# The recurrent mixer of the second block: one inversion of all small blocks, and four solving chains in lock step

## The chip, the cores and the metric

The kernel runs on one core of one Trainium2 chip. What counts is the device time of one execution in microseconds (us); the median of three runs stands for a kernel. One more execution was taken with the profiler, and all durations below come from it. The TensorE clock of the core has two levels here, 1.2 and 2.4 GHz; the profile gives the granted share of the higher one.

## The reference, cut to what matters

The program is a whole two-layer first block, then a second block. In the second block three parts share the input: a recurrent mixer (RWKV-7), a latent attention, and two gates over both. Their merge goes on to a router and 32 experts.

```python
def step(state, inp):                       # recurrent mixer, one token, 8 heads of 64
    r_t, w_t, k_t, v_t, kk_t, a_t = inp
    sa = jnp.einsum('bhvk,bhk->bhv', state, -kk_t)
    state = (state * w_t[:, :, None, :]
             + sa[..., None] * (kk_t * a_t)[:, :, None, :]
             + v_t[..., None] * k_t[:, :, None, :])
    return state, jnp.einsum('bhvk,bhk->bhv', state, r_t)
...
y = (y - mean) * lax.rsqrt(var + GN_EPS)    # per head, then weight and bias
y = (y + bonus) * g
...
merged = gate_rw * (y_rw @ w_branch_rw[l]) + gate_mla * (y_mla @ w_branch_mla[l])
x = x + merged @ w_out[l]
```

The kernel computes the 512 steps in 8 pieces of 64 tokens. Within a piece the tokens depend on each other through a unit triangular 64x64 matrix per head, whose inverse is needed; it is put together from the inverses of its two diagonal 32x32 blocks and one correction. With 8 heads, 8 pieces and 2 blocks there are 128 such small blocks. Between pieces a 64x64 state is carried on.

## The kernel before

Two heads share a tile of 128 partitions, so there are four chains, numbered `ct` 0 to 3.

`prepare` (L1307) makes a chain's operands in two halves of 4 pieces each, so it runs eight times: decay sums and exponentials, `KR` and its partners, products between them on the PE (L1292), transposes (L126), evictions split between ScalarE and VectorE (L1402, L1404). After the second half it stores the chain's triangular matrices (`nd`, L1376) and loads their 32 small blocks as rows of the tile `NB` (L1381), one block a partition: chain `ct` has partitions 32 ct to 32 ct + 31.

`invert` (L1415) inverts the blocks of two chains, so 64 partitions, by 31 steps of two VectorE instructions: an outer product (L1422) and a subtraction (L1424), of up to 256 elements a partition. It then stores the inverses to DRAM (`xbd`, L1427, a DMA that GpSimd's queue issues) and loads them as blocks into the tiles `TT` (L1433, four loads a chain, on the sync queue SP). It is written as a generator, and the caller advances it between other steps: chains 0 and 1 are inverted during the last four runs of `prepare`, chains 2 and 3 while chains 0 and 1 are solved.

`solve` (L1437) takes one chain from the inverses to the output. It loads `rt`, `bon` and `gg`; transposes the first blocks (`T1`, L1454); makes the off-diagonal block by two rounds of 32x32 products (L1460, L1470); multiplies the inverse with `R` (wide products through `products`, L1292), which gives `W` and `Zn`; makes `Phi`, `Psi`, `rt`; then runs the recursion over 6 pieces (product in `pairmm`, L1285, sum on VectorE, L1501); makes `y` (L1507, L1509, L1512); and normalises it with two products with `mean64` (L1515, L1523), a logarithm and an exponential on ScalarE (L1524, L1525), and seven VectorE passes, of which the last splits `y` into two parts, `yrh` and `yrl` (L359, L360). It yields after each step.

`merge_work` (L1556) is the work that depends on none of this: 4 projections of gate columns, then 4 latents with a gate projection and a product with the latent attention's output; in all 80 steps of 6 products (L188 to L190), 480 products of 128x512. VectorE evicts gates at L1538 and merges latents at L1551, which GpSimd's queue stores (L1552, L1559). The first 54 steps (`FREE`, L1296) are free to run at any time. The other 26 are bound: `solve_pair` (L1565) goes round its two chains, and after every second solving step ties one step of six products behind that solving step (`issue_after`, L1578). Chains 0 and 1 are solved first, then 2 and 3 (L1611, L1614).

The order of the instructions on each engine is made by a scheduler at build time from this program order; on the chip each engine takes its instructions in that order. Behind the mixer comes the merge: 96 products with `w_branch_rw` (L1672 to L1674), 48 of which need chains 0 and 1 and 48 chains 2 and 3, then the output projection, the router and the experts.

Of the kernel before, what the change touches and what calls it, by code (L numbers as in the profile page):

```python
# [9 lines left out]
F32 = mybir.dt.float32  # L10
# [5 lines left out]
OP = mybir.AluOpType  # L16
PSUM = bass.MemoryType.PSUM

T = 512
# [62 lines left out]
def build(tc, A, out):  # L82
    nc = tc.nc
# [24 lines left out]
    tt = nc.vector.tensor_tensor  # L108
# [1165 lines left out]
    def rwkv():  # L1274
        with tc.tile_pool(name="rw", bufs=1) as rp:
# [138 lines left out]

            def invert(cts, eng):  # L1415

                rows = slice(32 * cts[0], 32 * cts[0] + 64)
                N_, X_ = NB[rows], XB[rows]
                for j in range(31):
                    n_ = 31 - j  # L1420
                    o = outer[rows, :(j + 1) * n_].rearrange("p (s t) -> p s t", t=n_)
                    eng.tensor_tensor(o, X_[:, 0:j + 1, j:j + 1].to_broadcast([64, j + 1, n_]),  # L1422
                       N_[:, j:j + 1, j + 1:].to_broadcast([64, j + 1, n_]), OP.mult)
                    eng.tensor_tensor(X_[:, 0:j + 1, j + 1:], X_[:, 0:j + 1, j + 1:], o, OP.subtract)  # L1424
                    yield
                xbd = scratch.tile([64, 32, 32], F32, name=f"xbd{cts[0]}")
                nc.gpsimd.dma_start(xbd, X_)  # L1427
                for i, ct in enumerate(cts):
                    for h in range(2):
                        for hb in range(2):  # L1430
                            r0 = 64 * h + 32 * hb
                            p0 = 32 * i + 16 * h + 8 * hb
                            nc.sync.dma_start(TT[ct][r0:r0 + 32, :, 32 * hb:32 * hb + 32],  # L1433
                                                xbd[p0:p0 + 8].rearrange("c s t -> s c t"))
                yield

            def solve(sp, ct):  # L1437
# [4 lines left out]

                def tmp(nm):
                    return sp.tile([128, T], F32, tag=f"stmp{ct % 2}", name=nm, bufs=5)

                def load(nm, src):
                    t_ = sp.tile([128, T], F32, tag="s_" + nm, name=nm, bufs=2)
                    nc.sync.dma_start(t_, src)
                    return t_
                rt = c8(load("rt", rtd[ct].rearrange("p c t -> p (c t)")))  # L1450
                bon, gg = load("bon", bond[ct]), load("gg", ggd[ct])
                t_ = tmp("T1")
                T1, Z2 = c8(t_[:, 0:256]), c8(t_[:, 256:])
# [21 lines left out]

                W = c8(tmp("W"))
                Zn = c8(tmp("Zn"))
                for hf in range(2):
# [5 lines left out]
                    act(Zn[:, 4 * hf:4 * hf + 4], pv[:, :, 1], AF.Copy, scale=-1.0)  # L1484
                Phi = c8(tmp("Phi"))
                tt(Phi, id2[:, None].to_broadcast([128, 8, 64]), dec[:, :, None].to_broadcast([128, 8, 64]),
                   OP.mult)
                yield last
                for l_, r_, dst, op in ((W, Btok, Phi, OP.subtract), (Btok, Zn, Psi, OP.add),
# [4 lines left out]
                    yield last  # L1494
                M = c8(tmp("M"))
                nc.vector.tensor_copy(M[:, 1], Psi[:, 0])
# [13 lines left out]

                y = tmp("y")
                tt(c8(y), c8(p), Y0, OP.add)  # L1512
# [3 lines left out]
                tt(y, y, pm, OP.subtract)  # L1516
                sq = tmp("sq")
                sqi = act(sq, y, AF.Square)
# [45 lines left out]

            def solve_pair(a, b, side, steps):  # L1565

                nonlocal todo
                gens = [a, b]
                while gens:
                    for g in list(gens):  # L1570
                        last = next(g, None)
                        if last is None:
                            gens.remove(g)
                            continue
                        todo += RATE
                        while todo >= 1.0:
                            todo -= 1.0
                            with tc.issue_after(last.ins):  # L1578
                                next(work, None)
                        for _ in range(steps):  # L1580
                            next(side, None)
            outer = rp.tile([128, 256], F32, name="outer")
# [14 lines left out]
            with tc.tile_pool(name="rw_prepare", bufs=1) as pp:  # L1597
                inv = invert((0, 1), nc.vector)
                for i in range(8):
                    for _ in prepare(pp, i // 2, i % 2):  # L1600
                        if i >= 4:
                            next(inv, None)
                            next(inv, None)
                for _ in inv:
                    pass
            for _ in range(FREE):
                next(work)
            with tc.tile_pool(name="rw_solve", bufs=1) as sp:
                inverse_tiles(sp, (2, 3))
                inv = invert((2, 3), nc.vector)  # L1610
                solve_pair(solve(sp, 0), solve(sp, 1), inv, 2)  # L1611
                for _ in inv:
                    pass
                solve_pair(solve(sp, 2), solve(sp, 3), iter(()), 0)  # L1614
            for _ in work:
# [517 lines left out]
```

## Time and profile before

| | |
|---|---|
| median of three runs | 2293.4 us (2291.48 to 2294.9) |
| the profiled execution | 2294.18 us, span of the trace 2292.4 us |
| busy over the span | PE 2110.6 us (92%), weight loads 1661.8, VectorE 1691.4 (74%), ScalarE 1312.1, GpSimd 701.2 |
| the preparation | 1600 to 1729 us from the start of the span |
| solving | 1730 to 1829 us |
| merge of the branches | 1829 to 1853 us |
| experts | from about 1940 us |

PE is TensorE's matmul part, PEld its weight loads, DVE VectorE, ACT ScalarE, POOL GpSimd, SP the sync engine, which only issues DMAs. Times of events count from the start of the span. The ends of matmuls are modelled in the trace, so their spacing (from start to start) is read, not their duration. A `q` behind an engine's name is its queue of waits and DMA issues.

### The profile page before, as it was taken

How to read it: one execution, taken by the hardware profiler on the slowest of the kernel's cores; microseconds unless marked ns; L12 is line 12 of the kernel's file. 1: busy time of each engine (PE TensorE's matmuls, PEld its weight loads, DVE VectorE, ACT ScalarE, POOL GpSimd, SP SyncE). 2: the span in 40 equal slices, each digit the busy share in tenths (PEclk: the TensorE clock that was granted, in tenths of full speed). 3: DMA queues.
4: the chain of work that ended last, by engine and by line, in shares of the span. 5: the costliest groups of instructions: out<-in, count | busy, mean ns of one | idle time of the engine just before them, and what ended most of it. 6: DMA issues, size and time to landing. Idle time of an engine off the chain costs nothing. (4 is left out here: it accounts for less than half of the span.)

```text
span 2292.4 us, 31372 instructions
## 1 busy us (share of the span) xinstructions
PE 2110.6 (92%) x11354; PEld 1661.8 (72%) x11354; DVE 1691.4 (74%) x2725; ACT 1312.1 (57%) x2018; POOL 701.2 (31%) x620
## 2 busy tenths in 40 slices
PE   7798899999999799899999998999899996999995
PEld 6676688778777677678777876577667775777663
DVE  6888884766686888894676685475697565899897
ACT  4454664544555345764555456776763433888884
POOL 1343421233232444421223232332232042222214
PEclk9999999999999899899999999999999997999997
DMA  5211218566633112127666636556786695999992
GB/s 149 63 56 45 78 47 221 153 159 166 169 89 124 38 56 83 53 40 222 169 156 154 174 84 177 146 116 171 208 198 163 176 345 179 315 321 333 312 341 115
DMA packets 236547, 364.56 MB, mean 159 GB/s; under 512 B 46983, under 2 KB 135431, under 8 KB 234336
## 3 DMA queue, kind: packets, MB, share of 16 engines
q1 hardware_dynamic: 183952, 270.96, 36.3%
q0 software_dynamic: 32048, 84.30, 17.0%
q10 hardware_dynamic: 20384, 7.21, 1.3%
q8 instruction: 92, 1.51, 0.3%
q14 instruction: 71, 0.58, 0.1%
HBM read 302.78 MB, written 40.14 MB: 150 GB/s over the span
## 5 line engine op out<-in xcount | busy, mean ns | idle before, releaser
L879 DVE TENSOR_TENSOR wlo<-draw,whi 128x1024 fp32r<-128x1024 f32 x112 | 189.4, 1694 | 165.0 <-ACT whi L878 165.0
L161 ACT ACTIVATE whi<-wraw 128x1024 fp32r<-128x1024 f32 x171 | 179.2, 1054 | 203.5 <-PE ps_g L189 87.9
L1985 DVE TENSOR_TENSOR wlo<-eraw,whi 128x1024 fp32r<-128x1024 f32 x190 | 229.7, 1235 | 34.5 <-ACT whi L1984 31.0
L167 DVE TENSOR_TENSOR wlo<-wraw,whi 128x1024 fp32r<-128x1024 f32 x132 | 171.8, 1307 | 60.3 <-ACT whi L161 59.8
L1984 ACT ACTIVATE whi<-eraw 128x1024 fp32r<-128x1024 f32 x190 | 197.2, 1072 | 30.9 <-PE ps_s L1910 22.4
L188 PE MATMUL ps_g<-uh,whi 128*128 128x512 f32 x512 | 199.7, 390 | 0.0
L190 PE MATMUL ps_g<-uh,wlo 128*128 128x512 f32 x512 | 199.7, 390 | 0.0
L189 PE MATMUL ps_g<-ul,whi 128*128 128x512 f32 x512 | 199.6, 390 | 0.0
L878 ACT ACTIVATE whi<-draw 128x1024 fp32r<-128x1024 f32 x112 | 118.1, 1054 | 103.8 <-PE ps_g L189 73.3
L190 PE MATMUL ps_g<-h2h,wlo 128*128 128x512 f32 (+1 forms) x288 | 117.8, 410 | 2.5 <-DMA wlo<-wraw 2.5
L188 PE MATMUL ps_g<-hhh,whi 128*128 128x512 f32 x288 | 117.3, 408 | 2.0 <-ACT whi L170 1.8
L188 PE MATMUL ps_g<-h2h,whi 128*128 128x512 f32 (+1 forms) x288 | 118.8, 413 | 0.3 <-DMA wlo<-wraw 0.3
L189 PE MATMUL ps_g<-h2l,whi 128*128 128x512 f32 (+1 forms) x288 | 117.8, 409 | 0.0
L190 PE MATMUL ps_g<-hhh,wlo 128*128 128x512 f32 x288 | 117.6, 408 | 0.0
L189 PE MATMUL ps_g<-hhl,whi 128*128 128x512 f32 x288 | 116.2, 404 | 0.0
L563 POOL TENSOR_TENSOR KE<-Dm,kk 128x512 f32<-128x512 f32 x56 | 78.0, 1403 | 108.5 <-ACT Dm L561 63.5
L188 PEld LDWEIGHTS ps_g<-uh,whi 128*128 128x128 f32 x512 | 96.2, 188 | 20.3
L190 PEld LDWEIGHTS ps_g<-uh,wlo 128*128 128x128 f32 x512 | 96.2, 188 | 20.2
L189 PEld LDWEIGHTS ps_g<-ul,whi 128*128 128x128 f32 x512 | 96.2, 188 | 20.0
L840 ACT ACTIVATE ar<-ps_g 128x512 f32<-128x512 f32 x64 | 38.0, 593 | 125.6 <-PE ps_g L190 125.6
L854 POOL DMA_DIRECT2D draw<-in_w_down_dram x16 | 21.2, 1327 | 285.9 <-DMA draw<-in_w_down_dram 127.1
L1909 PE MATMUL ps_s<-wlo,xth 128*104 128x512 f32 x256 | 105.7, 413 | 2.0 <-DVE wlo L1985 1.8
(774 smaller groups left out, 6185.5 us busy)
## 6 DMA issues: line engine op xcount, KB each, us to landing
eraw<-in_moe_w_gu_dram SPq DMA_DIRECT2D x61, 1024.0 KB, 17.7
draw<-in_w_down_dram SPq DMA_DIRECT2D x40, 1024.0 KB, 5.9
wraw<-in_w_in_dram SPq DMA_DIRECT2D x74, 512.0 KB, 3.8
wraw<-in_w_up_dram SPq DMA_DIRECT2D x64, 512.0 KB, 5.2
eraw<-in_moe_w_down_dram SPq DMA_DIRECT2D x30, 1024.0 KB, 17.8
wlo<-wraw POOLq DMA_DIRECT2D x39, 512.0 KB, 5.5
draw<-in_w_down_dram POOLq DMA_DIRECT2D x16, 1024.0 KB, 9.3
draw<-draw POOLq DMA_DIRECT2D x16, 1024.0 KB, 7.1
```

The costliest lines, as they stand in the source:

```text
L161: act(hv, rv, AF.Copy)
L167: tt(lv, rv, f32(hv), OP.subtract)
L188: mm(o, hi[:, j, cs], xh, start=(k == 0), stop=False)
L189: mm(o, hi[:, j, cs], xl, start=False, stop=False)
L190: mm(o, lo[:, j, cs], xh, start=False, stop=(k == K - 1))
L563: nc.gpsimd.tensor_tensor(KE, Dm.rearrange("p c b u m -> p (c b u m)"), kk, OP.mult)
L840: act(ar[:, 2 * s:2 * s + 2, c], p.rearrange("p (i t) -> p i t", i=2), AF.Relu)
L878: act(hi, rv, AF.Copy)
L879: tt(lo, rv, f32(hi), OP.subtract)
L1909: mm(pg, XTh[:, k], lo[:, j], start=False, stop=False)
L1984: act(hi, rv, AF.Copy)
L1985: tt(lo, rv, f32(hi), OP.subtract)
```

## The change

All 128 blocks are inverted by one pass of 62 instructions over 128 partitions, after the whole preparation and ahead of the free steps of `merge_work` in program order. The inverses are stored by two DMAs and loaded by sixteen. All four chains are then solved in one round. Each chain has two tiles of its own (`tp`, `my`) in place of five from a ring: `W` and `Zn` are written into `R`, `T1`, `Z2`, `Phi` and the squares share `tp`, `M` and `y` share `my`. `rt` has four buffers, `bon` and `gg` keep two for four chains.

```diff
-            def invert(cts, eng):
-                rows = slice(32 * cts[0], 32 * cts[0] + 64)
-                N_, X_ = NB[rows], XB[rows]
+            def invert():
                 for j in range(31):
                     n_ = 31 - j
-                    o = outer[rows, :(j + 1) * n_].rearrange("p (s t) -> p s t", t=n_)
-                    eng.tensor_tensor(o, X_[:, 0:j + 1, j:j + 1].to_broadcast([64, j + 1, n_]),
-                       N_[:, j:j + 1, j + 1:].to_broadcast([64, j + 1, n_]), OP.mult)
-                    eng.tensor_tensor(X_[:, 0:j + 1, j + 1:], X_[:, 0:j + 1, j + 1:], o, OP.subtract)
-                    yield
-                xbd = scratch.tile([64, 32, 32], F32, name=f"xbd{cts[0]}")
-                nc.gpsimd.dma_start(xbd, X_)
-                for i, ct in enumerate(cts):
+                    o = outer[:, :(j + 1) * n_].rearrange("p (s t) -> p s t", t=n_)
+                    tt(o, XB[:, 0:j + 1, j:j + 1].to_broadcast([128, j + 1, n_]),
+                       NB[:, j:j + 1, j + 1:].to_broadcast([128, j + 1, n_]), OP.mult)
+                    tt(XB[:, 0:j + 1, j + 1:], XB[:, 0:j + 1, j + 1:], o, OP.subtract)
+                xbd = scratch.tile([128, 32, 32], F32, name="xbd")
+                for i in range(2):
+                    nc.gpsimd.dma_start(xbd[64 * i:64 * i + 64], XB[64 * i:64 * i + 64])
+                for ct in range(4):
...
-                def load(nm, src):
-                    t_ = sp.tile([128, T], F32, tag="s_" + nm, name=nm, bufs=2)
+                t_, my = [sp.tile([128, T], F32, name=f"{nm}{ct}") for nm in ("tp", "my")]
+                def load(nm, src, bufs):
+                    t_ = sp.tile([128, T], F32, tag="s_" + nm, name=nm, bufs=bufs)
...
-                rt = c8(load("rt", rtd[ct].rearrange("p c t -> p (c t)")))
-                bon, gg = load("bon", bond[ct]), load("gg", ggd[ct])
-                t_ = tmp("T1")
+                rt = c8(load("rt", rtd[ct].rearrange("p c t -> p (c t)"), 4))
+                bon, gg = load("bon", bond[ct], 2), load("gg", ggd[ct], 2)
...
-                W = c8(tmp("W"))
-                Zn = c8(tmp("Zn"))
+                W, Zn = R[:, :, 0], R[:, :, 1]
...
-            def solve_pair(a, b, side, steps):
+            def solve_all(gens):
                 nonlocal todo
-                gens = [a, b]
...
-                        for _ in range(steps):
-                            next(side, None)
...
             with tc.tile_pool(name="rw_prepare", bufs=1) as pp:
-                inv = invert((0, 1), nc.vector)
                 for i in range(8):
                     for _ in prepare(pp, i // 2, i % 2):
-                        if i >= 4:
-                            next(inv, None)
-                            next(inv, None)
-                for _ in inv:
-                    pass
-            for _ in range(FREE):
-                next(work)
+                        pass
             with tc.tile_pool(name="rw_solve", bufs=1) as sp:
                 inverse_tiles(sp, (2, 3))
-                inv = invert((2, 3), nc.vector)
-                solve_pair(solve(sp, 0), solve(sp, 1), inv, 2)
-                for _ in inv:
-                    pass
-                solve_pair(solve(sp, 2), solve(sp, 3), iter(()), 0)
+                invert()
+                for _ in range(FREE):
+                    next(work)
+                solve_all([solve(sp, ct) for ct in range(4)])
```

The lines above shift by a few in the changed kernel: the outer product is L1420 there, the subtraction L1422, the gate eviction L1532, the latent's merge L1545, the first block product L1455, the second L1465, the loads of a chain L1444. Three places show what the scheduler made of it.

On VectorE, in the preparation of the third chain, before (a row is the line, the operation, output and inputs, and the output's shape; `SB` and `SK` are evictions of the preparation, `outer` and `inverses` the inversion):

```order
L1340 SCALAR_TENSOR_TENSOR kk<-zk,k_k,sq 128x256
L1424 TENSOR_TENSOR inverses<-inverses,outer 64x4x28
L1371 TENSOR_TENSOR SB_12862<-ps_m,past 128x512
L1422 TENSOR_TENSOR outer<-inverses,blocks 64x135
L1371 TENSOR_TENSOR SK<-ps_m,past 128x512
L1424 TENSOR_TENSOR inverses<-inverses,outer 64x5x27
L1385 TENSOR_TENSOR km<-km,dec_12866 128x256
```

and now, at the end of the preparation:

```order
L1404 COPY KV<-ps_m 64x2x64 x2
L1404 COPY Btok_12869<-ps_m 64x2x64 x2
L1532 TENSOR_TENSOR gate<-ps_g,Rb_10846 128x512
L1545 SCALAR_TENSOR_TENSOR gate<-gate,ps_g 128x512 x2
L1420 TENSOR_TENSOR outer<-inverses,blocks 128x31
L1422 TENSOR_TENSOR inverses<-inverses,outer 128x31
L1420 TENSOR_TENSOR outer<-inverses,blocks 128x60
```

The inversion no longer alternates with the preparation; its 62 instructions stand behind it and behind the first latent's merges, with two gate evictions between them and the transposes of `TT` behind.

On the PE, at the start of solving, now (`ymh`, `yml` and `wlo` are operands of work products, `tp` the transposed blocks of a chain; 71 work products in a row end with the first three rows, where before there were 37):

```order
L188 MATMUL ps_g<-ymh,whi 128x512
L189 MATMUL ps_g<-yml,whi 128x512
L190 MATMUL ps_g<-ymh,wlo 128x512
L1455 MATMUL ps_s<-tp_14476,SB_12852 32x32 x16
L1455 MATMUL ps_m<-tp_14504,SB_12857 32x32 x16
...
L1455 MATMUL ps_s<-tp_14538,SB_12862 32x32 x16
L1465 MATMUL ps_s<-TT_12893,tp_14476 32x32 x16
L1465 MATMUL ps_s<-TT_13905,tp_14538 32x32 x16
L1292 MATMUL ps_s<-R_12853,TT_12893 64x128 x11
L1455 MATMUL ps_m<-tp_14566,SB_12867 32x32 x16
```

Where "..." stands are six work products. All four chains' first products now follow the free work; six work products stand between most pairs of steps from there on, and after the last pair the eight products with `mean64` and the merge follow with none between.

On the sync queue, where the merge's operands are loaded, now (`gates` takes the stored gates `gd` and latents `partd`; `bon` and `gg` are the bonus and output gate of chains 2 and 3):

```order
L1643 DMA gates<-gd 128x512 x2
L155 DMA wraw<-in_w_out_dram 128x2x512 x2
L1643 DMA gates<-partd 128x512 x2
L1444 DMA bon<-bond 128x512 x2
L1444 DMA gg<-ggd 128x512 x2
L1757 DMA yd<-zero 128x1024 x2
```

Before, those four loads stood directly behind the loads of `TT` for chains 2 and 3, ahead of all loads of `gates`.

## Rows read from the trace of the kernel before

**Rows 1.** Busy time by stretch: each engine busy (instructions), clock, DMA share, GB/s.

```profile
core 0: us, PE busy (x) PEld busy (x) DVE busy (x) ACT busy (x) POOL busy (x), PEclk, DMA share, GB/s
1621.20:1626.60 5.40, 5.37 (x37) 4.78 (x38) 3.73 (x8) 3.66 (x5) 2.08 (x4) 0.50 1.07 276
...
1621.00:1685.00 64.00, 62.44 (x588) 49.20 (x588) 50.51 (x138) 51.64 (x109) 21.48 (x37) 0.95 0.73 188
1685.00:1730.00 45.00, 40.15 (x368) 30.90 (x368) 40.75 (x126) 25.56 (x56) 17.39 (x26) 1.00 0.78 186
...
1940.00:2230.00 290.00, 286.79 (x1382) 203.74 (x1381) 261.42 (x302) 255.47 (x360) 71.02 (x56) 1.00 0.95 322
```

**Rows 2.** Waits of the PE, 1685 to 1730: us in total, times, longest.

```profile
PE ps_m L1292 <- ACT KV L1402: 1.9, 3, 1.2
PE ps_m L1292 <- DVE za L1364: 1.7, 1, 1.7
PE ps_m L1292 <- ACT y0b L1411: 1.2, 1, 1.2
```

**Rows 3.** Waits of the PE, 1738 to 1828.

```profile
PE ps_s L1285 <- DVE M L1501: 1.2, 2, 0.7
```

**Rows 4.** Timeline of the PE: start, duration, engine, line, operation, count.

```profile
1729.04 0.28 PE L1292 MATMUL ps_m<-KV,SK 64*64 64x64 f32 x2
...
1737.52 0.39 PE L188 MATMUL ps_g<-ymh,whi 128*128 128x512 f32 x1
1737.74 0.40 PE L189 MATMUL ps_g<-yml,whi 128*128 128x512 f32 x1
1738.07 0.69 PE L1460 MATMUL ps_s<-T,SB 32*32 32x32 f32 x32
```

**Rows 5.** Timeline of GpSimd's queue: stores of the inverses, loads of the blocks.

```profile
1723.68 0.57 POOL L1427 DMA_DIRECT2D xbd<-inverses  x1 [2.29 <-DVE inverses L1424]
1724.27 2.73 POOL L1381 DMA_DIRECT2D blocks<-nd  x4
...
1777.14 0.58 POOL L1427 DMA_DIRECT2D xbd<-inverses  x1 [8.78 <-DVE M L1501]
```

**Rows 6.** DMAs by tile: queue, count, size, median us from issue to landing.

```profile
partd<-gate POOLq DMA_DIRECT2D x8, 256.0 KB, 4.3
...
bon<-bond SPq DMA_DIRECT2D x4, 256.0 KB, 4.5
blocks<-nd POOLq DMA_DIRECT2D x16, 32.0 KB, 4.9
```

**Rows 7.** VectorE by line, 1737.9 to 1777: busy us, mean ns, idle before.

```profile
L1424 DVE TENSOR_TENSOR inverses<-inverses,outer 64x31 f32<-64x31 f32 (+15 forms) x31 | 10.5, 339 | 1.0
L1422 DVE TENSOR_TENSOR outer<-inverses,blocks 64x31 f32<-64x31 f32 (+15 forms) x31 | 10.5, 339 | 1.0
```

**Rows 8.** Timeline of VectorE: transposes of chains 0, 1 and 2.

```profile
1730.80 0.45 DVE L1454 STREAM_TRANSPOSE T<-TT 128x256 f32<-128x256 f32 x1 [3.51 <-DMA TT<-xbd]
1735.03 0.45 DVE L1454 STREAM_TRANSPOSE T<-TT 128x256 f32<-128x256 f32 x1 [3.78 <-DMA TT<-xbd]
...
1785.99 0.44 DVE L1454 STREAM_TRANSPOSE T<-TT 128x256 f32<-128x256 f32 x1
```

**Rows 9.** Timeline of the sync queue: loads of the blocks, chains 0 and 1.

```profile
1726.72 4.83 SPq L1433 DMA_DIRECT2D TT<-xbd  x8
```

**Rows 10.** Timeline of the PE: first wide products of chain 0 and of chain 2.

```profile
1742.24 3.60 PE L1292 MATMUL ps_s<-R,TT 64*64 64x128 f32 x31 [0.79 <-ACT TT L1473]
...
1795.88 2.04 PE L1292 MATMUL ps_s<-R,TT 64*64 64x128 f32 x31
```

**Rows 11.** Timeline of the PE: mean products of chains 0 and 1.

```profile
1784.32 1.02 PE L1515 MATMUL ps_s<-y,mean 128*128 128x512 f32 x2
1785.18 1.02 PE L1515 MATMUL ps_m<-y,mean 128*128 128x512 f32 x2
```

**Rows 12.** Timeline of VectorE: splits that end chains 0 and 1.

```profile
1795.65 0.69 DVE L360 TENSOR_TENSOR yrl<-y,yrh 128x512 fp32r<-128x512 f32 x1 [0.45 <-ACT yrh L359]
...
1798.12 0.69 DVE L360 TENSOR_TENSOR yrl<-y,yrh 128x512 fp32r<-128x512 f32 x1 [0.57 <-ACT yrh L359]
```

More of the change, by code (lines that the diff above doesn't have):

```diff
@@ L1431, in invert @@
                             r0 = 64 * h + 32 * hb
-                            p0 = 32 * i + 16 * h + 8 * hb
+                            p0 = 32 * ct + 16 * h + 8 * hb
                             nc.sync.dma_start(TT[ct][r0:r0 + 32, :, 32 * hb:32 * hb + 32],
                                                 xbd[p0:p0 + 8].rearrange("c s t -> s c t"))
-                yield
             def solve(sp, ct):
@@ L1441, in solve @@
                 tag = "sm"[ct % 2]
-                def tmp(nm):
-                    return sp.tile([128, T], F32, tag=f"stmp{ct % 2}", name=nm, bufs=5)
-                def load(nm, src):
-                    t_ = sp.tile([128, T], F32, tag="s_" + nm, name=nm, bufs=2)
+                t_, my = [sp.tile([128, T], F32, name=f"{nm}{ct}") for nm in ("tp", "my")]
+                def load(nm, src, bufs):
+                    t_ = sp.tile([128, T], F32, tag="s_" + nm, name=nm, bufs=bufs)
                     nc.sync.dma_start(t_, src)
                     return t_
-                rt = c8(load("rt", rtd[ct].rearrange("p c t -> p (c t)")))
-                bon, gg = load("bon", bond[ct]), load("gg", ggd[ct])
-                t_ = tmp("T1")
+                rt = c8(load("rt", rtd[ct].rearrange("p c t -> p (c t)"), 4))
+                bon, gg = load("bon", bond[ct], 2), load("gg", ggd[ct], 2)
                 T1, Z2 = c8(t_[:, 0:256]), c8(t_[:, 256:])
@@ L1484, in solve @@
                     act(Zn[:, 4 * hf:4 * hf + 4], pv[:, :, 1], AF.Copy, scale=-1.0)
-                Phi = c8(tmp("Phi"))
+                Phi = c8(t_)
                 tt(Phi, id2[:, None].to_broadcast([128, 8, 64]), dec[:, :, None].to_broadcast([128, 8, 64]),
@@ L1494, in solve @@
                     yield last
-                M = c8(tmp("M"))
+                M = c8(my)
                 nc.vector.tensor_copy(M[:, 1], Psi[:, 0])
@@ L1509, in solve @@
                             last = mm(o, M[h, c], rt[h, c], start=False, stop=True)
-                y = tmp("y")
+                y = my
                 tt(c8(y), c8(p), Y0, OP.add)
@@ L1516, in solve @@
                 tt(y, y, pm, OP.subtract)
-                sq = tmp("sq")
+                sq = t_
                 sqi = act(sq, y, AF.Square)
```

## The prediction

> **What bounds the kernel now.** I read five views in this order: busy time by stage, TensorE's waits, the timelines of PE, VectorE and the two DMA-issuing queues around the inversions, and the table of transfers. In the stage of the change the PE is nearly full. While the first five half-chains are prepared it is busy 62.44 of 64 us; in the stretch where the first inversion is woven into the preparation it is busy 40.15 of 45 us, and VectorE 40.75 [rows 1]. The PE's waits there are 1.9 + 1.2 on ScalarE's evictions and 1.7 on VectorE, 4.8 us in all [rows 2]; the evictions wait in turn for VectorE's copies. The second inversion runs beside the solving of chains 0 and 1 and costs the PE 1.2 us of waits in the recursion [rows 3]. So VectorE's second pass of 62 instructions costs the PE little. It can stay so cheap because the PE holds a store of products that depend on nothing here, the gate and latent projections (called work products below; 480 of them, 0.23 us apart [rows 4]). They run down to the instant at which the first solving product can start: the last work product is issued at 1737.74 and the first block product at 1738.07, with no wait between [rows 4].
>
> After the mixer comes the merge, the router and the experts. Between 1940 and 2230 us the PE is busy 286.79 of 290 us and the DMA 0.95 [rows 1]; the weights it streams go into buffers which the merge still holds, so a mixer that ends later moves all of that by the same amount.
>
> **The change, part by part.** My sum is made on the PE, against the profiled execution's own 2294.2 us, which stands 0.8 above the median of the runs.
>
> *One inversion less in the preparation.* 62 VectorE instructions leave the preparation. I take the 4.8 us of PE waits as gone, since the stretch without an inversion loses only 1.6 us in 64 [rows 1, 2]: **-4.8** (bounds -4.8 and 0).
>
> *Where the PE runs dry.* The preparation's last product ends at 1729.3 [rows 4]. Now it ends 4.8 earlier, and 6.1 earlier again because 26 work products that stood before it (94 then, 68 now, counted from the first place where the orders part) stand behind it: 1718.4. Behind it are 71 work products instead of 37: 71 x 0.233 = 16.5 us, to 1735.0. The next PE instruction is the first block product of chain 0, and every work product after the 324th is placed behind some solving step, so the PE, which takes its products in order, has nothing else.
>
> *When that product can start.* VectorE now begins the inversion after the two merges of the first latent (line 1551), which need the 11th of the 71 products: 1718.4 + 2.6 + two merges of 0.7 = 1722.5. The blocks are there by then: their loads were issued from 1724.27 for 2.73 us [rows 5], now some 10.9 earlier, and land 4.9 later [rows 6], so 1721.0. The second inversion took 10.5 us in each of its two lines with 1.0 of gaps each, 23.0 us over 64 partitions [rows 7]; the first, also over 64, was no dearer, and I take the same for 128. Two gate evictions stand inside it, 1.4 us: it ends at 1746.9. Then the result goes out to DRAM and comes back as blocks: from the store's issue at 1723.68 to chain 0's transpose at 1730.80 is 7.1 us, the other time 1777.14 to 1785.99, 8.9 us [rows 5, 8]; with two stores instead of one I take 8.0. The transpose and its hand-over are 0.6: 1755.5. The PE stands still from 1735.0 to 1755.5, **+20.5** (bounds 17.5 and 23).
>
> *Four chains' blocks instead of two.* Eight block loads took 4.83 us to issue, 0.6 each [rows 9], and chain 1's transpose came 4.2 after chain 0's [rows 8]. With sixteen loads in one row chain 3's last one goes out 7.2 us after chain 0's last. The PE has six work products (1.4 us) and some 3 us of block products for that time: **+3.0** (0 to 5.5).
>
> *Lock step.* Between two steps of a pair there are now twelve work products and the other pair instead of six, so the waits in the recursion and before the first wide products, 1.2 + 0.8, go [rows 3, 10]: **-2.0**. Work products and solving products are the same in number, so they cost nothing new. The chains' first wide products took 3.60 us in pair 0 against 2.04 in pair 1 [rows 10], where the PE had just had small products and waits; the new order has work products there: **-1.6**. Writing W and Zn into R and reusing one tile per chain costs nothing as far as I see: each eviction already waits for the products that read the place which it overwrites.
>
> *The clock.* Behind the stop before the first half-chain's products the granted clock was 0.50 for 5.4 us [rows 1]: 1.2 of 2.4 GHz, so half of that time is lost. So the long idle costs a further **+2.7** (0 to 2.7). The Trainium skill (TensorE: Matmul & The Clock Gate, Part 1) says that an idle PE falls back to half clock and only sustained activity releases it; by that rule the second idle below would also cost 2.7, and the sum would be 1.3 more. For that second, shorter idle I take half the price, **+1.4**.
>
> *The end.* Pair 0's normalisation ran behind pair 1's first products, and pair 1's behind the 48 merge products of the first two chains. Now all four end together and the merge waits for the first pair. From the first mean product (1784.32) to the end of the first split is 12.0 us, to that of the second 14.5 [rows 11, 12]. The PE has eight such mean products meanwhile, 0.86 apart [rows 11] and so about 7.2 us. That leaves 4.8 us at least; with the other two chains' subtractions and squares on VectorE and ScalarE between them, four of 0.69, 10.1 at most. I take **+7.0**. Chains 2 and 3 are covered by the 48 merge products, 11.2 us.
>
> The sum: -4.8 + 20.5 + 3.0 - 2.0 - 1.6 + 2.7 + 1.4 + 7.0 = **+26.2 us**, 2320.4 on the profiled execution's scale, **2319.6 us** as a median.
>
> **Rivals.**
>
> 1. *VectorE's time is what counts: faster.* If the work products reached to the first block product, only the gains would be left: -4.8 - 2.0 - 1.6 = -8.4, so 2285. Against it: from 1718.4 to 1755.5 are 37.1 us, which take 159 products at 0.233, and 71 are there. It decides only if the inversion and its trip took under 16.5 us, less than the inversion alone in [rows 7]. The Trainium skill (Trainium Kernel Development and Optimization, Best Practices) says to tile to 128 partitions always; a kernel bound by VectorE would gain 22 us of its time by that, and [rows 2, 3] show that this one isn't. Chance 0.05.
>
> 2. *The idle before the solving comes, the one at the end does not*, because the first pair's end is carried by products that are issued late: 26.2 - 7.0 - 1.4 = +17.8, 2311. For it: single rows of the tail overlap well in [rows 12]. Against: no work product is left behind the last solving step. Chance 0.19.
>
> 3. *The new order of the sync queue holds chains 2 and 3.* Their bonus and gate operands are now loaded behind the last two loads of the stored latents, which must first be written (4.3 us) and whose own issue waits; then the bonus lands in 4.5 [rows 6] and it also needs chain 0 to let go of the buffer. By my count they are in some 18 us after the last work product and chain 3 is ready at 24.5, against 25.2 when the 48 merge products end: covered by a hair. Each microsecond later is paid; a second landing would make +8, 2328. Chance 0.10.
>
> 4. *The slip is absorbed later* by the experts' stage if its weight stream, not the PE, bounded it [rows 1]; then 2293, no change. Against: the first loads wait for the merge's own buffers. Chance 0.03.
>
> **How the numbers follow.** The forecast has the rest, 0.63. Changes under 0.2% (4.6 us), about what a measurement of this kernel can tell from none, fall to rival 4. All low ends of the terms together give +13.9, 2307; all high ends would give nearly +40, which I cut at 2331, where rival 3 lies inside. With the low side widened a little for rival 2 the range is 2304 to 2331; it leaves out rivals 1 and 4 and the far ends. Faster 0.05, same 0.03, slower 0.92.
>
> **What would show it.** In the new trace: no PE wait over 1 us during the preparation; a gap of 18 to 23 us on the PE directly before the first 32x32 block product, ended by the transposes; 62 inversion instructions with 128 partitions at the same mean as before, 21 us busy in all; a granted clock of 0.5 for some us behind the gap; no waits in the recursion; a second gap of 5 to 10 us between the last mean product and the first merge product; and the same distance as before from the last merge product to the end. I am wrong if the PE still has work products when the blocks come back, if the gap is under 10 us, or if the experts' stage takes the slip back.

## The result and the profile after

The changed kernel takes 2315.0 us in the median of four runs (2310.8 to 2323.1) against 2294.2 of the kernel before on the same chip: ratio 1.0102, 95% interval 1.0082 to 1.0121, or about 21 us slower. Timed twice more it took 2315.4 (1.0106, 1.0091 to 1.0120) and 2315.0 (1.0104, 1.0083 to 1.0124). The forecast was 2319.6, slower.

Its profiled execution is the slowest of the four, 2323.1 us with a span of 2321.3. Busy time by stretch, with the columns of [rows 1]:

```profile
1621.00:1685.00 64.00, 60.71 (x584) 48.02 (x584) 50.96 (x138) 51.85 (x107) 20.66 (x37) 0.95 0.72 183
1685.00:1741.20 56.20, 52.43 (x415) 40.47 (x413) 37.91 (x102) 29.61 (x62) 18.75 (x27) 0.97 0.90 215
1741.20:1759.40 18.20, 0.03 (x1) 0.00 (x0) 10.65 (x31) 3.04 (x4) 1.99 (x3) 0.64 0.54 128
1759.40:1770.00 10.60, 9.58 (x184) 8.21 (x186) 2.63 (x5) 3.76 (x10) 0.00 (x0) 0.50 0.24 37
1770.00:1780.00 10.00, 10.00 (x117) 7.40 (x114) 2.39 (x4) 4.59 (x9) 2.02 (x3) 0.50 0.21 68
...
1800.00:1850.00 50.00, 50.00 (x701) 38.32 (x698) 21.57 (x51) 9.27 (x11) 3.96 (x6) 1.00 0.53 161
...
1857.50:1862.60 5.10, 0.00 (x0) 0.00 (x0) 4.70 (x9) 3.73 (x8) 0.00 (x0) 0.65 0.73 287
1862.60:1887.00 24.40, 24.37 (x100) 19.68 (x101) 15.74 (x24) 6.70 (x9) 7.79 (x10) 0.93 0.71 239
...
1960.00:2250.00 290.00, 280.85 (x1344) 200.08 (x1345) 254.99 (x295) 250.45 (x352) 75.09 (x59) 0.97 0.93 312
```

TensorE (PE) stands still for 18.2 us, works on at half clock, is full from 1800 to 1850, in the lock step (50.00 of 50 us), and stops again for 5.1 us. Its waits from 1690 to 1960 give both stops, and for the second what ended it (us in total, times, longest):

```profile
PE ps_s L1455 <- issue: 18.2, 1, 18.2
...
PE ps_g L1655 <- ACT yrh L359: 5.3, 1, 5.3
PE ps_g L190 <- DMA wlo<-wraw: 2.9, 1, 2.9
...
PE ps_m L1517 <- ACT tp L1512: 1.3, 2, 0.8
PE ps_m L1292 <- ACT KV L1402: 0.8, 3, 0.3
PE ps_m L1455 <- DVE tp L1449: 0.7, 1, 0.7
PE ps_s L1465 <- issue: 0.2, 1, 0.2
```

L1455 is the first 32x32 block product, L1655 the first merge product, L1517 the second mean product. The preparation's waits (L1292) are 0.8 us where [rows 2] had 4.8; those of the recursion, [rows 3], are gone. The timeline of the PE around the first stop answers to [rows 4]:

```profile
1719.56 0.51 PE L1292 MATMUL ps_m<-KV,SK 64*64 64x64 f32 x10
...
1733.13 1.22 PE L190 MATMUL ps_g<-h2h,wlo 128*128 128x512 f32 x2 [2.87 <-DMA wlo<-wraw]
...
1740.84 0.39 PE L190 MATMUL ps_g<-ymh,wlo 128*128 128x512 f32 x1
1759.46 1.06 PE L1455 MATMUL ps_s<-tp,SB 32*32 32x32 f32 x32 [18.24 <-issue]
1761.24 1.06 PE L1455 MATMUL ps_m<-tp,SB 32*32 32x32 f32 x32 [0.72 <-DVE tp L1449]
```

The last work product is issued at 1740.84. What the PE waits for is read on VectorE. By line, from 1724.5 to 1752.9 (answers to [rows 7]):

```profile
L1422 DVE TENSOR_TENSOR inverses<-inverses,outer 128x31 f32<-128x31 f32 (+15 forms) x31 | 10.6, 343 | 1.0
L1420 DVE TENSOR_TENSOR outer<-inverses,blocks 128x31 f32<-128x31 f32 (+15 forms) x31 | 10.6, 342 | 2.5 <-DMA blocks<-nd 1.5
L1532 DVE TENSOR_TENSOR gate<-ps_g,Rb 128x512 f32<-128x512 f32 x2 | 1.4, 688 | 2.9 <-PE ps_g L190 2.9
```

An instruction over 128 partitions takes 342 to 343 ns in the mean, over 64 it took 339 [rows 7]: the blocks of the second inversion are done at no further cost, which frees 21 us of VectorE's time. But the one inversion now starts late, and its timeline shows a second thing:

```profile
1722.23 1.36 DVE L1545 SCALAR_TENSOR_TENSOR gate<-gate,ps_g 128x512 f32<-128x512 f32 x2 [5.06 <-PE ps_g L190]
1725.08 0.19 DVE L1420 TENSOR_TENSOR outer<-inverses,blocks 128x31 f32<-128x31 f32 x1 [1.49 <-DMA blocks<-nd]
...
1738.74 0.69 DVE L1532 TENSOR_TENSOR gate<-ps_g,Rb 128x512 f32<-128x512 f32 x1 [2.94 <-PE ps_g L190]
```

The inversion starts at 1725.08, when the blocks of the last chain land, and stands for 2.94 us behind a gate eviction, which waits for a PE that waits 2.87 us for the weight `wlo` (a wait of the PE that [rows 4] did not have; it stands among the 71 work products). The result goes out and comes back on two queues (answers to [rows 5, 9]), GpSimd's first:

```profile
1716.05 2.71 POOL L1381 DMA_DIRECT2D blocks<-nd  x4 [2.77 <-DMA nd<-SB]
...
1752.70 1.14 POOL L1425 DMA_DIRECT2D xbd<-inverses  x2 [6.66 <-DVE inverses L1422]
```

```profile
1755.66 9.00 SPq L1431 DMA_DIRECT2D TT<-xbd  x16
```

How far the changed kernel is behind the one before, at five places in the program (start of the instruction, or the span's end; the second pair of columns is a second profile of the changed kernel, 2311.7 us, from the experiments):

| place | before | after | behind | after, 2nd | behind |
|---|---|---|---|---|---|
| last product of the preparation | 1729.04 | 1719.56 | -9.5 | 1718.96 | -10.1 |
| first block product | 1738.07 | 1759.46 | +21.4 | 1757.55 | +19.5 |
| first merge product | 1829.03 | 1862.63 | +33.6 | 1854.98 | +26.0 |
| last merge product | 1853.12 | 1885.92 | +32.8 | 1879.66 | +26.5 |
| end | 2292.4 | 2321.3 | +28.9 | 2309.9 | +17.5 |

Behind the last merge product some is given back. The kernel before had these PE waits in the output projection (its waits, 1852 to 1945):

```profile
PE ps_g L228 <- DVE mg L363: 1.7, 2, 1.2
...
PE ps_g L227 <- DVE wlo L167: 1.4, 1, 1.4
PE ps_g L226 <- DVE gates L1677: 0.2, 1, 0.2
```

Together 3.3 us; the changed kernel has none of the three. Its second stop, just ahead of the merge, gives the loads and VectorE time to get ahead, which would explain it: with two pairs (below) that stop is gone and the three waits are back. No run tests it by itself.

The rest lies further on. From the first transposes of an expert's middle values (`ga`: 1947.72 before, 1977.64 and 1970.47 after) to the end are 344.7 us before, 343.7 in the first profile after and 339.4 in the second. Two executions of one kernel differ there by 4.3 us, so what of it belongs to the change stays open; the executions of the kernel before alone range from 2286 to 2298 us. (One more took 2826 us at a granted clock of 0.68 and is left out.)

### The profile page after: what moved, and what is told of

Same layout as the page of the kernel before. It is cut to its first block, busy times and chain, and to the rows that moved or that the text cites. A ratio compares the mean times of both kernels' runs of the same rounds, so it can differ in the third digit from the quotient of the medians.

```text
span 2321.3 us, 31299 instructions
## 1 busy us (share of the span) xinstructions
PE 2118.6 (91%) x11354; PEld 1666.4 (72%) x11354; DVE 1671.2 (72%) x2663; ACT 1312.5 (57%) x2018; POOL 698.6 (30%) x620
## 5 line engine op out<-in xcount | busy, mean ns | idle before, releaser
L879 DVE TENSOR_TENSOR wlo<-draw,whi 128x1024 fp32r<-128x1024 f32 x112 | 188.4, 1685 | 165.0 <-ACT whi L878 165.0
## 6 DMA issues: line engine op xcount, KB each, us to landing
eraw<-in_moe_w_gu_dram SPq DMA_DIRECT2D x61, 1024.0 KB, 17.5
```

What stands on the lines that cost most here:

```text
L879: tt(lo, rv, f32(hi), OP.subtract)
```

## The experiments

Eleven runs. Times stand beside runs of the kernel before on the same chip.

### The changed kernel again

No edit. First:

> The changed kernel once more, nothing edited, to see what of its profile repeats. Theory: the idle time of 18.2 us ahead of the first 32x32 block product, the 6.6 us of waits around the mean products and the 5.3 us ahead of the merge come back within 1 us; the median is 2311 to 2319. Open: the profile at hand (2323.1) is 8 us above the median of its runs and shows a granted clock of 0.50 for some 22 us behind the idle stretch. If that stretch has a fixed length, it stands in this profile too; if its length varies, a shorter one goes with a time nearer to 2315, by about half a microsecond per microsecond.

Measured: 2315.4 us (before 2291.8). Both stops come back: 18.3 and 5.3 + 1.3 us (the 6.6 of the expectation has the 5.3 in it). The long low clock does not: it lasted 10.5 us in this profile, and the clock returned with the PE as busy as in the profile shown above (columns of [rows 1]):

```profile
1757.50:1768.00 10.50, 9.67 (x186) 8.29 (x187) 2.63 (x5) 3.74 (x10) 0.00 (x0) 0.50 0.24 38
1768.00:1772.00 4.00, 4.00 (x78) 3.02 (x75) 1.57 (x3) 2.47 (x5) 0.59 (x1) 0.88 0.00 0
```

And beside the last group:

> The changed kernel beside the two others, as the measure for them: 2313 to 2317, with an idle time of 18.3 us and between 9 and 24 us at half clock behind it.

Measured: 2315.0 us (before 2290.3), stops of 18.0 and 5.2 us, and this time, in an execution of 2322.0, the long form:

```profile
1759.90:1784.00 24.10, 23.04 (x312) 18.03 (x314) 5.39 (x9) 8.77 (x20) 2.02 (x3) 0.50 0.28 61
```

So the length varies, 10.5 to 24 us, and the profiles with the long form are of the two longest executions, 2323.1 and 2322.0.

### More free products for the stop

```diff
-            FREE, RATE = 54, 0.5
+            FREE, RATE = 66, 0.26
```

> 66 instead of 54 steps of work products are free of the solving steps (72 products more, 72 x 0.233 = 16.8 us), and the rest is spread at 0.26 a step instead of 0.5. Theory (TensorE has nothing to do while the one late inversion and its trip run): the idle time of 18.2 us falls to 1 to 4 us, the low clock behind it goes too, and the time falls by 17 to 25 us, to 2290 to 2298, unless the solving with fewer products between its steps waits more, which would show as waits in its recursion. Rival (lock step and operands in place are what costs): the products only move, what the idle time loses the recursion's waits gain, 2310 to 2316. Rival (the idle time counts, the clock does not): 2315 - 16.8 = 2298.

Measured: 2300.2 us (ratio 1.0042, 1.0029 to 1.0054), 15.1 below the changed kernel beside it, and above the 2290 to 2298 expected. The recursion gets no waits from having fewer products between its steps. The stop is 10.0 us shorter, but 8.3 us of it are left, not 1 to 4, and the low clock behind it stays (0.55 in the mean from 1764 to 1774):

```profile
PE ps_s L1455 <- DMA TT<-xbd: 8.3, 1, 8.3
PE ps_g L1655 <- ACT yrh L359: 5.3, 1, 5.3
```

Nor is the stop all of the gain. The products are the same in number, but between solving steps they cost more. Starts of groups of six in the recursion, first in the second profile of the changed kernel (two groups for sixteen 64x64 products), then with 66 free steps (one group for sixteen):

```profile
1806.82 0.50 PE L188 MATMUL ps_g<-ymh,whi 128*128 128x512 f32 x1
...
1810.75 0.50 PE L188 MATMUL ps_g<-h2h,whi 128*128 128x512 f32 x1
```

```profile
1804.62 0.50 PE L188 MATMUL ps_g<-h2h,whi 128*128 128x512 f32 x1
...
1806.83 0.50 PE L188 MATMUL ps_g<-h2h,whi 128*128 128x512 f32 x1
```

That is 3.93 us against 2.21, so a group adds 1.72 us where six products in a row take 1.40 (6 x 0.233). Twelve groups moved, which makes some 3.9 us, an estimate from these rows: the stop accounts for 10.0 of the 15.1 us, and some 4 are saved in the lock step.

Why 8.3 us are left, stands in the trip of the inverses. In the changed kernel it takes 6.2 us from the store's issue to the first transpose of blocks. GpSimd's queue and VectorE in the second profile of the changed kernel:

```profile
1750.73 1.14 POOL L1425 DMA_DIRECT2D xbd<-inverses  x2 [5.30 <-DVE inverses L1422]
...
1756.90 0.45 DVE L1449 STREAM_TRANSPOSE tp<-TT 128x256 f32<-128x256 f32 x1 [6.46 <-DMA TT<-xbd]
```

With 66 free steps it takes 11.9, while the weights of the further products are loaded. GpSimd's queue, the sync queue and VectorE there:

```profile
1751.34 1.14 POOL L1425 DMA_DIRECT2D xbd<-inverses  x2 [2.96 <-DVE inverses L1422]
...
1757.07 0.37 SPq L155 DMA_DIRECT2D wraw<-in_w_branch_rw_dram  x1
1757.88 9.53 SPq L1431 DMA_DIRECT2D TT<-xbd  x16
...
1763.29 0.45 DVE L1449 STREAM_TRANSPOSE tp<-TT 128x256 f32<-128x256 f32 x1 [9.69 <-DMA TT<-xbd]
```

The DMA share during the trip is 1.06 instead of 0.64 (stretches 1751.3 to 1763.3, and 1750.7 to 1756.9 of the changed kernel), and the loads also stand behind a weight load that waits for its buffer, though what they wait for last is the store's landing (0.3 us). The Trainium skill (DMA: Bandwidth & Descriptors, Latency and other measured facts) says that the fixed cost of a transfer rises with the load on the memory. The direction agrees: a load of blocks lands 2.0 us behind its issue in the changed kernel and 3.1 us here, in the median, and the whole trip doubles; but no run changed the load on the memory alone.

### One inversion, but two pairs

```diff
-                solve_all([solve(sp, ct) for ct in range(4)])
+                for a in (0, 2):
+                    solve_all([solve(sp, ct) for ct in (a, a + 1)])
```

> One inversion of all 128 blocks as in the change, but the chains solved in two pairs, 0 and 1, then 2 and 3. Theory: the idle time of 18 us stays, since it lies ahead of all solving; the end does not stop, since the second pair and the merge products of the first cover it: the 5.3 + 1.3 us of waits around the last mean products go, some waits of about 1.2 us in all come back in the recursion, and the time is 2309 to 2312. Rival (the lock step saves more than its end costs): slower than the changed kernel, 2316 to 2320. Rival (the whole slip is the lock step's): 2294.

Measured: 2308.1 us (1.0065, 1.0052 to 1.0079), 7.3 below the changed kernel beside it, a little more than expected. Its waits of the PE, 1690 to 1905:

```profile
PE ps_s L1455 <- issue: 18.0, 1, 18.0
...
PE ps_g L228 <- DVE mg L363: 2.3, 2, 1.2
PE ps_g L227 <- DVE wlo L167: 1.4, 1, 1.4
PE ps_s L1465 <- ACT tp L1458: 0.9, 2, 0.6
```

The first stop is untouched, no wait is left on the first merge product or the mean products, and the waits in the output projection are back, 3.9 us as against 3.3 in the kernel before, so that a part of what the end saves is lost there. (This profile is of its longest execution, 2316.5 us.)

### What the clock costs

Behind the last free work product, products that nobody reads keep the PE busy; they are work beyond what the reference needs:

```diff
+                with tc.issue_after(newest[0].ins):
+                    p = ps("g")
+                    for _ in range(76):
+                        mm(p, YMh[:, 0, 0:128], YMh[:, 0], start=True, stop=True)
                 solve_all([solve(sp, ct) for ct in range(4)])
```

> Behind the last free work product stand 76 products of 128x512 into a tile that nobody reads (76 x 0.233 = 17.7 us), so TensorE waits as long for the inverses but is busy meanwhile; it is work beyond what the reference needs. Theory: the first block product starts when it did, and the granted clock is 1.0 behind it instead of 0.50. If the low clock costs what the prediction gave it, 2.7 us, the time is 2312; if it costs what the profile at hand shows (some 22 us at half clock with TensorE nearly full), 2305 or less. Rival (the 32x32 and 64x64 products themselves are granted half the clock, idle stretch or not): the clock of 0.50 stays and the time is 2315.

Measured: 2315.5 us, no change, and the granted clock was low all the same:

```profile
1740.00:1757.70 17.70, 17.70 (x79) 14.34 (x77) 10.62 (x31) 3.05 (x4) 1.99 (x3) 1.00 0.60 166
1759.20:1770.00 10.80, 9.68 (x188) 8.33 (x188) 2.63 (x5) 4.14 (x12) 0.00 (x0) 0.54 0.23 36
```

Between the unused products and the first block product were 1.54 us of idle time, and 0.82 behind it. Either that was enough, or it was the small products. So the same with 88:

> 88 unused products of 128x512 instead of 76, so that they reach past the moment at which the inverses are back and TensorE goes from them to the first block product with no idle time; that product comes some 1.2 us later than it could. If the wait of 1.54 us in the run with 76 is what lowered the clock, the granted clock is now 1.0 until the next wait; if it falls to 0.50 within 5 us behind the first block products all the same, the idle time is not its cause here.

Measured: 2308.0 us in its one execution, and the clock stays up through the same solving products:

```profile
1759.30:1771.00 11.70, 11.16 (x298) 8.98 (x298) 4.41 (x8) 8.03 (x18) 1.15 (x2) 1.00 0.27 66
```

> The kernel with 88 unused products once more, now timed, since its one look showed the clock at 1.0 behind the idle stretch and 2308.0 us. Theory (the wait, however short, brings TensorE to half clock for some 10 us, which costs 5 us): 2308 to 2311, 4 to 7 us below the changed kernel timed beside it. Rival (the one look was a low run; with 76 products the time did not move either): 2314 to 2316.

Measured: 2311.2 us, 3.7 below the changed kernel beside it (1.0091, 1.0072 to 1.0109, against 1.0104, 1.0083 to 1.0124); the clock in that profile was again 1.00, though its execution took 2319.0 us. The intervals overlap, so the times alone don't show a saving, but the traces give the price. From the first block product to the first merge product are 92.7 us with the clock kept up (1759.33 to 1852.03; 93.05 in the second such profile), 97.4 with the short low stretch (1757.55 to 1854.98) and 103.2 with the long one (1759.46 to 1862.63). Of the differences, 0.3 and 0.5 us are waits between the first block products, so the half clock costs some 4.4 us or 10.0 us. The Trainium skill (TensorE: Matmul & The Clock Gate, Part 1) lets idle time lower the clock and sustained activity release it. The runs agree with the first: clock low behind the idle time, 1.00 without it. The stretch of 24.1 us at 0.50 with the PE busy for 23.04 of them doesn't agree with the second, and the measurement decides.

The kernel before shows it too. Its first wide products took 3.60 us against 2.04 in the second pair [rows 10], behind waits of 0.3, 0.2 and 0.8 us, and while they ran the granted clock was down at 0.50:

```profile
1744.00:1746.00 2.00, 2.00 (x22) 2.00 (x20) 1.83 (x6) 0.66 (x2) 0.00 (x0) 0.50 0.94 220
```

With the clock kept up (88 unused products) the same 31 products took 1.52 + 0.76 us, in the second profile of the changed kernel 2.82 + 0.76; the first part with the clock up, and that of the changed kernel's first profile:

```profile
1764.38 1.52 PE L1292 MATMUL ps_s<-R,TT 64*64 64x128 f32 x22
```

```profile
1768.06 2.82 PE L1292 MATMUL ps_s<-R,TT 64*64 64x128 f32 x22
```

### Both causes at once

66 free steps and two pairs, both edits as above:

> Both edits of the earlier two runs together: 66 free steps of work products and the chains solved in two pairs. If the two causes (TensorE out of free products, and the common end of four chains) are separate and add up, the gain of the pairs, 7 us, comes on top of the 2300: 2293, the time of the kernel before. Rival (with few products between its steps a pair waits in its recursion, which four chains in lock step would not): 2296 to 2300, with waits of 3 us and more in the recursion.

Measured: 2299.2 us (1.0034, 1.0021 to 1.0047): 6.8 above the kernel before, where 66 free steps alone were 8.4 above. The gains don't add up, and the time is the rival's; its mechanism came true in part. The pairs, with few products between their steps, wait 3.0 us, not in the recursion but in the block products, the wide products and the step behind it (1.5 + 0.5 + 1.0), 2.1 in the output projection, and the stop was 10.8 us instead of 8.3. (Its profile is of its longest execution, 2306.7 us.)

Then chains 2 and 3 five rounds behind chains 0 and 1, and the loads of the blocks on two queues:

```diff
-            FREE, RATE = 54, 0.5
+            FREE, RATE = 66, 0.26
...
-                            nc.sync.dma_start(TT[ct][r0:r0 + 32, :, 32 * hb:32 * hb + 32],
+                            (nc.gpsimd, nc.sync)[ct // 2].dma_start(TT[ct][r0:r0 + 32, :, 32 * hb:32 * hb + 32],
...
                 while gens:
+                    if (rounds := rounds - 1) == 0: gens += later
...
-                solve_all([solve(sp, ct) for ct in range(4)])
+                solve_all([solve(sp, ct) for ct in range(2)], [solve(sp, ct) for ct in (2, 3)], 5)
```

> 66 free steps; chains 2 and 3 begin five rounds of solving steps behind chains 0 and 1, so that the recursions overlap but the ends do not; and the loads of the inverted blocks of chains 0 and 1 go out on GpSimd's queue, right behind the store, instead of the sync queue, where with 66 free steps they stood 3.5 us behind a weight load that waited for its buffer. Theory: the idle time ahead of the first block product is 8.3 - 3.5 = 4.8 us, the waits around the end are under 1.5 us instead of 5.6: 2300 - 3.5 - 5.5 = 2291. Rival (the loads are bound by the store's landing, not by their queue): 2294.5.

Measured: 2301.9 us (1.0042, 1.0026 to 1.0058); both forecasts missed. The end is covered, but the stop is 8.9 us: on GpSimd's queue the loads waited 5.2 us for the store to land, then took 4.7 in the median to land themselves instead of 2.0, at a DMA share of 1.04 and 1.00 (1750 to 1760, 1760 to 1770). The queue was not what held them. And 4.6 us of waits came back in the output projection.

Two pairs, the same queue, 70 free steps at 0.19:

> 70 free steps (24 products more than with 66, 5.6 us), two pairs, and the loads of chains 0 and 1 on GpSimd's queue. Theory: the idle time ahead of the first block product is 0 to 2 us; the end is covered; the time is 2286 to 2290 if the recursion waits under 3 us, that is below the kernel before by what the inversion saves in the preparation. Rival (each further free step puts a gate eviction and its wait for a weight into the inversion on VectorE and so moves the inverses by about as much): the idle time stays at 4 us or more, 2292 to 2296.

Measured: 2294.7 us, ratio 1.0008 (0.9992 to 1.0023): the time of the kernel before. The time lies in the rival's range; the stop is down to 3.0 us, between the two forecasts, and the trip still takes 12.1. With 20 unused products in that place:

> The two-pair kernel with 70 free steps, in which 3.0 us of idle time were left ahead of the first block product, with 20 unused products (4.7 us) in that place. Theory: the granted clock stays 1.0 where the first pair starts, about 10 us at half clock go, and the time falls by 3 to 5 us, to 2290 to 2292, level with or a little below the kernel before. Rival (its waits in the first pair's first steps lower the clock anyway): 2294 to 2297.

Measured: 2292.1 us, ratio 1.0005 (0.9993 to 1.0017). The clock was 1.00 through the first pair, yet the two ratios can't be told apart. No version found beats the kernel before: the 4.0 us of waits that the one inversion takes out of the preparation are lost again elsewhere.

## Why the prediction was right

The PE's account, term by term, in the second profile of the changed kernel (in brackets the first):

| step of the prediction | forecast | measured |
|---|---|---|
| one inversion less in the preparation | -4.8 | -4.0 (waits 4.8 to 0.8 in both) |
| where the PE runs dry, when that product can start | +20.5 | +18.3 (18.2; third timing 18.0) |
| the wait for `wlo` among the 71 work products | not in the sum | +2.9 (2.9) |
| four chains' blocks instead of two | +3.0 | +0.8 (0.9) |
| lock step, waits | -2.0 | -3.0, none left of 1.5 in the recursion, 0.8 and 0.7 ahead of it |
| lock step, wide products | -1.6 | -1.3 with the clock kept up (1.52 + 0.76 against 3.60); at half clock none (2.82 + 0.76) |
| the clock behind the long idle time | +2.7 | +4.4 (10.0) |
| the clock behind the second | +1.4 | +3.1 (1.7), half of 6.2 (3.3) us at 0.50 |
| the end | +7.0 | +6.6 (6.6), 5.3 + 1.3 |
| waits in the output projection | not in the sum | -3.3 (-3.3) |

Up to the last merge product the measured terms add up to +27.8, where the table of places has +26.5, so 1.3 us are not accounted for. With the output projection it is +24.5, against +21 to +25 in the three timings. That the forecast of +26.2 came so near owes something to luck: the stop and the blocks were forecast 4.4 us too high, the clock 3.4 too low, and two waits, +2.9 and -3.3, were missing.

*Right.* The argument that decided the sign: work products end while the one inversion and its trip still run, because nothing behind the 324th may go ahead of a solving step. Taking 72 products into the stop gave back 15.1 us, 10.0 of them in the stop itself. The end was sized well too, and taking the common end away gave 7.3.

*Where the PE runs dry* and *When that product can start* were both too early, in the first profile by 6.2 us (1735.0, measured 1741.2) and 4.0 us (1755.5, measured 1759.5). The difference came out nearly right because the errors partly have one source, the wait of 2.87 us for the weight. It stands among the 71 products, with some half-clock products behind it, and the preparation ended 1.6 us late (1720.0, not 1718.4). The inversion started at 1725.1, not 1722.5, since the last block loads were issued at 1716.05 where the step had 10.9 us taken off 1724.27; and the step counted the gate evictions inside it at their own 1.4 us, without the 2.94 that one of them waits for that PE. The trip was shorter, 6.1 us (6.2 in the second profile), not 8.0.

*The clock* is the term that was mis-sized: priced from a stretch of 5.4 us at 0.50 [rows 1], it lasted 10.5 or 24 us. And its premise was wrong in one point: the long idle time isn't needed, waits of 1.54 and 0.82 us did the same. *Four chains' blocks* was too dear: the other chains' loads landed while the PE worked, and with the clock kept up, from a start some 1.2 us later than possible, only 0.5 us of waits was left.

Of the forecasts on the profile, "no PE wait over 1 us during the preparation" holds from 1690 on; at the preparation's start the stop ahead of the first half-chain's products is 7.0 and 6.1 us long, where it was 5.4 before. "The same distance from the last merge product to the end" failed: 439.3 us before, 435.4 and 430.2 after. That is what remains of rival 4: the output projection took 3.3 us back, and the share of the experts' stage, 1.0 and 5.3 us in two executions of one kernel, stays open. Rival 1 fell with the stop of 18 us, and rival 2 with the second of 5.3. Rival 3 fell too: no PE wait stands between the first and the last merge product, 24.37 of 24.40 us busy.

## What to carry to other kernels

Merging two passes into one over twice the partitions halved the instructions here at no cost for each (342 ns against 339), but it makes all users wait for the last input; ask first what the bottleneck engine can still do from its last free instruction to the new, single hand-over. Free work that is moved into such a gap brings its transfers along; here the very trip that one waits for took twice as long beside them. When chains run in lock step, price their common end: what covered the tail of one was the body of the next.

## What was not expected of the hardware

- A wait of 1.54 us ahead of the small products, and one of 0.82 between them, brought 10.8 us at a mean granted clock of 0.54, about as much as a stop of 18.3 us (10.5 us at 0.50); without the two waits (one of 0.50 was left) the same products ran at 1.00.
- The low stretch had two lengths in one kernel, 10.5 and 24.1 us, with the PE busy for 92% and 96% of it. What decides between them is open; it accounts for 5.8 us between two executions (103.2 and 97.4 from the first block product to the first merge product).
- The trip of the inverses through DRAM, from the store's issue to the first transpose, took 6.2 us at a DMA share of 0.64 and 11.9 at 1.06. That the other transfers are the cause is the reading of the traces; no run changed them by themselves.
- Six work products in a row took 1.40 us, between two recursion steps 1.72.
